# Bringing transposed value heads back in one DMA, and planning for a longer round trip

## The chip, the cores and the metric

The kernel runs on one core of a Trainium2 chip, in one launch. The metric is the device time of a run in microseconds (us). The kernel before takes 1620.33 us (median of 3 runs, 1620.0 to 1620.79).

The core has a matrix engine (TensorE, PE in the profile; its weight loads are listed as PEld), three engines for elementwise work (VectorE or DVE, ScalarE or ACT, GpSimd or POOL), and SyncE (SP), which here does nothing but issue DMAs. Each engine runs its own instructions in the order in which they stand in its program. A wait at the head of an engine's queue therefore holds up everything behind it.

## The reference

One layer of a decoder trunk on 512 tokens of width 1024, in float32:

```python
h = x + 0.5 * swiglu(rmsnorm(x, ffn1_norm), ffn1_w_in, ffn1_w_out)
h = h + hybrid_mixer(rmsnorm(h, mix_norm), w_in, ...)
h = h + 0.5 * swiglu(rmsnorm(h, ffn2_norm), ffn2_w_in, ffn2_w_out)
return rmsnorm(h, final_norm)
```

The mixer has one wide input projection whose columns feed two recurrent branches. The branch that matters here is Gated DeltaNet: 8 heads of queries and keys and 16 heads of values, each 128 wide. Values go through a causal convolution over 4 tokens and a SiLU, and then into a chunked delta rule:

```python
qkv = silu(causal_short_conv(concatenate([gq, gk, gv], -1), conv_w))
cq, ck, cv = split(qkv, [1024, 2048], -1)
# per value head, in chunks:
u = matmul(T, v * beta[..., None])
# scan over the chunks
v_new = u_c - w_c @ S
o = (q_c * exp(gam_c)) @ S + qk_c @ v_new
S = S * exp(g_end) + k_to_end.T @ v_new
```

The other branch (HGRN2, 8 heads) has a recurrence of its own. Both are projected back to 1024 columns, merged by sigmoid gates and projected once more.

## The kernel before, in words

**Stages.** The first feed-forward block takes the time up to about 362 us of the profiled span, the mixer runs to about 1265 us, and the second feed-forward block and the last norm take the rest. Every product is made of three float32r matmuls (high by high, high by low, low by high parts, L189 to L191), so each weight slab that arrives as `raw` is split by ACT into a high part (L1773) and by DVE into a low part (L1775).

**The mixer's order.** The mixer's instructions are put in order by a planner, the class `Desk`. The code is written as threads (Python generators). A thread asks for an engine for a stated time, for a buffer, for an event, or for a "lag", a time that passes in the plan without any engine. The planner runs its own clock and gives each engine to the waiting thread of the best rank. The order in which it serves the threads becomes the program order on every engine. The lags stand for transfers: `LAG["turn"]` for one way of a round trip through DRAM, `LAG["out"]` for a write to DRAM whose buffer comes free afterwards. A lag puts no wait into the program. The waits on the chip are semaphores that follow the data, whatever the plan thought.

**Threads.** `product` keeps PE busy with the dense projections. `loader` chooses which projection comes next, from a list (`DENSE`) as far as its needs are met, and otherwise from 16 gate products ("t"), which have no needs. It also holds back convolutions while seven of them are under way. The recurrence of head pair u (0 to 7) has the parts `g_n` (Gram products `pgq`, L1214), `g_b` (a triangular inverse of 32 by 32 blocks on POOL, which begins with four loads `gfs<-nb`, L1253), `g_inv` (the inverse of larger blocks, with transposes at L1284, L1291 and L1348), `g_w` (values times beta, L1273) and `g_rec` (the scan, which starts with the products `pw`, L1406).

**Values.** For each of the 16 value heads the projection leaves the head as 128 channels on the partitions by 512 tokens in a PSUM bank. `conv` takes two of the six buffers named `ta`, scales the product into one (`ci`, L1097), which frees the bank, and then convolves and applies the SiLU on ACT and DVE (L1102 to L1117). The scan wants tokens on the partitions. `turn` transposes blocks of 32 by 32 on DVE (L1126). `bounce` then writes the tile to DRAM (`vn<-ci`, 256 KB, L1132) and reads it back with the blocks in place (`gvb<-vn` or `x<-vn`, L1138): four DMAs of 64 KB, one for each group of 32 destination partitions. In both directions SP issues the DMAs, between the loads of weights (L1731) and the writes of other tiles (L1487, in `keep`). In the plan the `ta` buffer comes free after the first lag, and the head counts as finished after the second. `g_w` (L1273, on DVE) is the first reader.

The two banks for dense products (`mm`) are shared by all projections. The banks, the six `ta` buffers and the three buffers for `raw` are counted by the planner and guarded by semaphores on the chip.

Of the kernel before, what the change touches and what calls it, by code (L numbers as in the profile page):

```python
# [18 lines left out]
NT = T // P  # L19
# [29 lines left out]
STAY = (15,)  # L49
CONVS = 7  # L50
SLACK = 0.8
LAG = dict(raw=3.5, gb=6.5, nb=6, m=7, out=5, back=6, turn=2.5)
EASE = 2.5
LANES = {"a": 2, "b": 2, "d": 1, "e": 1}

# [632 lines left out]
def mixer(tc, mp, e):  # L688
    nc = tc.nc
    pe, act, dve, pool, sp = nc.tensor, nc.scalar, nc.vector, nc.gpsimd, nc.sync  # L690
# [73 lines left out]
    S = ("use", "SP", 0.4)  # L764
# [11 lines left out]
    def decays(pab):  # L776
# [74 lines left out]
        sp.dma_start(gtd, gt)  # L851
        yield "lag", LAG["out"]
        D.fire("decays")
# [237 lines left out]
    def conv(k, i, pt, out, n):  # L1091
# [21 lines left out]
        if n:  # L1113
            dve.scalar_tensor_tensor(out, a, 1.0, b, op0=ALU.add, op1=ALU.mult)
            D.put("ta", 2)
        else:
            dve.scalar_tensor_tensor(y, a, 1.0, b, op0=ALU.add, op1=ALU.mult)  # L1117
            yield V(512)
            turn(th, y)
            D.put("ta")  # L1120
            yield from bounce(f"vn{i}", th, out, "ta")
        D.fire(k)

    def turn(out, x):

        dve.transpose(out.rearrange("p (f c j) -> p c f j", f=4, c=NT), x)  # L1126

    def bounce(name, x, out, tag=None):

        yield S  # L1130
        scr = dr.tile([P, T], F32, name=name)
        sp.dma_start(scr, x)  # L1132
        yield "lag", LAG["turn"]
        if tag:
            D.put(tag)
        for f in range(4):
            yield S
            sp.dma_start(out[32 * f:32 * f + 32].rearrange("p (r a) -> p r a", r=4),  # L1138
                         scr.rearrange("(r i) (f a) -> f i r a", i=32, f=4)[f])
        yield "lag", LAG["turn"]  # L1140

    def g_e(u, st):
# [3 lines left out]
        for i in range(2):  # L1146
# [4 lines left out]
            act.dma_start(gb, gtd[hd_:hd_ + 1].rearrange("o (c b) -> o c b", c=NT).to_broadcast([P, NT, P]))  # L1151
            yield "lag", LAG["gb"]
            a = G["at"][u % 4 * 2 + i]
# [85 lines left out]
    def g_b(u, st):  # L1239
# [4 lines left out]
        for b in range(4):  # L1244
            r = slice(32 * b, 32 * b + 32)
            yield S
            sp.dma_start(nb[b].rearrange("s i j -> i s j"), n2[r, :, :, r].rearrange("p a c j -> p (a c) j"))
        yield "lag", LAG["nb"]
        yield "on", *([("P", u - 1)] if u else ["m"])
# [9 lines left out]
        sp.dma_start(t, eye4)  # L1259
        yield "lag", LAG["m"]  # L1260
        for j in range(31):
# [736 lines left out]
```

## Time and profile before

| | us |
|---|---|
| median of 3 runs | 1620.33 |
| lowest and highest | 1620.0 and 1620.79 |
| the profiled execution | 1619.26 |
| its span, first to last instruction | 1617.5 |
| outside the span | 1.76 |

A row of a group of instructions reads: engine, operation, out<-in by the program's names, count, then the durations in ns (least, median, most) and the first and last start. In a timeline the first two columns are start and duration in us, and a bracket at the end gives the idle time of the engine just ahead of the instruction and what ended it. In the table by windows each row is one stretch: its bounds, its length, the busy time of each engine with its instructions, the clock granted to TensorE as a share of full speed, the share of the DMA engines and GB/s. In a list of waits the columns are the total in us, the number of times, and the longest.

### The profile page before, as it was taken

The page shows a single profiled execution, that of the slowest core. Times are in us where ns is not written, and L with a number is a line of the kernel's source. Part 1 is how long each engine was busy: PE and PEld are TensorE (multiplying, and loading weights), DVE is VectorE, ACT ScalarE, POOL GpSimd, SP SyncE. Part 2 cuts the span into 40 slices and gives each one's busy share as a digit, 9 for nine tenths or more (in the row PEclk, how much of TensorE's full clock was granted, in tenths as well). Part 3 has the DMA queues.
Part 4 walks back from the last instruction along what each step waited for, and adds up shares of the span by engine and source line. Part 5 has one row for each costly group of instructions (what it writes and reads, how often), then busy time and mean ns, then how long its engine had stood idle before and what let it go on. Part 6 is the DMA issues. An engine that isn't in the chain of part 4 may idle for free.

```text
span 1617.5 us, 29307 instructions
## 1 busy us (share of the span) xinstructions
PE 1593.9 (99%) x10608; PEld 1380.8 (85%) x10608; DVE 1156.3 (71%) x2275; ACT 831.3 (51%) x1872; POOL 413.0 (26%) x725
## 2 busy tenths in 40 slices
PE   9999999999999999999998999999999999999997
PEld 8999998888888888888886787788888899999887
DVE  6888885447787788679887888765545788888433
ACT  5666664233434436456665665564324566667222
POOL 0211221001121121356555456600001121121001
PEclk9999999999999999999999999999999999999998
DMA  5777863332321322554343335446544587786333
GB/s 185 170 159 158 182 158 104 114 115 79 105 60 54 105 79 86 156 157 118 104 140 121 113 118 159 148 137 195 164 143 130 132 180 159 157 181 151 93 89 117
DMA packets 133345, 213.30 MB, mean 132 GB/s; under 512 B 22464, under 2 KB 36544, under 8 KB 133200
## 3 DMA queue, kind: packets, MB, share of 16 engines
q1 hardware_dynamic: 116208, 180.80, 37.2%
q0 software_dynamic: 14400, 26.22, 10.5%
q10 hardware_dynamic: 2592, 4.42, 0.9%
q8 instruction: 83, 1.36, 0.4%
q14 instruction: 62, 0.51, 0.1%
HBM read 192.21 MB, written 19.17 MB: 131 GB/s over the span
## 4 chain that ended last, share of the span: by engine, by line
PE 82%; DMA 8%; issue 6%; POOL 2%; DVE 1%; SPq 1%; ACT 1%; POOLq 0%; DVEq 0%; ACTq 0%
PE pmm L189 18%; PE pmm L190 17%; PE pmm L191 17%; PE px L191 5%; PE px L190 5%; PE px L189 5%; DMA wlo<-w1b 3%; DMA wlo<-w1a 2%; PE pnat L189 2%; PE pnat L191 2%; PE pnat L190 2%; PE pgq L1214 1%; DMA gvb<-vn 1%; PE pw L1406 1%; DMA vn<-ci 1%
## 5 line engine op out<-in xcount | busy, mean ns | idle before, releaser
L189 PE MATMUL pmm<-uh,whi 128*128 128x512 f32 x879 | 362.7, 413 | 3.1 <-DVE ci L1097 2.3
L191 PE MATMUL pmm<-uh,wlo 128*128 128x512 f32 x879 | 344.1, 391 | 0.0
L190 PE MATMUL pmm<-ul,whi 128*128 128x512 f32 x879 | 342.8, 390 | 0.0
L191 PE MATMUL px<-xs,wlo 128*128 128x256 f32 x1008 | 285.8, 284 | 1.2 <-DMA wlo<-w1b 0.6
L190 PE MATMUL px<-xs,whi 128*128 128x256 f32 x1008 | 285.3, 283 | 0.0
L189 PE MATMUL px<-xs,whi 128*128 128x256 f32 x1008 | 285.2, 283 | 0.0
L1773 ACT CAST whi<-raw 128x512 fp32r<-128x512 f32 x226 | 140.1, 621 | 231.3 <-PE pmm L190 182.1
L1775 DVE TENSOR_TENSOR wlo<-raw,whi 128x512 fp32r<-128x512 f32 x226 | 158.9, 705 | 108.8 <-ACT whi L1773 105.0
L191 PEld LDWEIGHTS pmm<-uh,wlo 128*128 128x128 f32 x879 | 165.4, 188 | 36.3
L189 PEld LDWEIGHTS pmm<-uh,whi 128*128 128x128 f32 x879 | 165.8, 189 | 35.4 <-DVE ci L1097 3.6
L191 PEld LDWEIGHTS px<-xs,wlo 128*128 128x128 f32 x1008 | 193.5, 192 | 2.2 <-DMA wlo<-w1b 1.3
L189 PEld LDWEIGHTS px<-xs,whi 128*128 128x128 f32 x1008 | 193.5, 192 | 0.1
L190 PEld LDWEIGHTS px<-xs,whi 128*128 128x128 f32 x1008 | 193.5, 192 | 0.1
L190 PEld LDWEIGHTS pmm<-ul,whi 128*128 128x128 f32 x879 | 166.1, 189 | 29.7 <-DVE ul L216 0.3
L329 ACT CAST whi<-sw 128x512 fp32r<-128x512 f32 x144 | 87.6, 613 | 92.7 <-DVE sw L366 72.7
L308 DVE TENSOR_TENSOR wlo<-raw,whi 128x512 fp32r<-128x512 f32 x100 | 77.6, 788 | 78.2 <-ACT whi L329 77.8
L329 ACT CAST whi<-raw 128x512 fp32r<-128x512 f32 x104 | 61.4, 592 | 127.4 <-PE pmm L190 91.7
L227 POOL TENSOR_TENSOR acc<-acc,sqt 128x512 f32<-128x512 f32 x18 | 23.4, 1300 | 320.2 <-ACT sqt L225 320.2
L308 DVE TENSOR_TENSOR wlo<-sw,whi 128x512 fp32r<-128x512 f32 x144 | 98.1, 681 | 0.0
L329 ACT CAST whi<-rw 128x512 fp32r<-128x512 f32 (+1 forms) x130 | 79.5, 613 | 26.5 <-PE px L190 14.5
L189 PE MATMUL pmm<-xs,whi 128*128 128x512 f32 (+1 forms) x238 | 89.8, 377 | 0.0
L190 PE MATMUL pmm<-xs,whi 128*128 128x512 f32 (+1 forms) x238 | 89.7, 377 | 0.0
(473 smaller groups left out, 3224.6 us busy)
## 6 DMA issues: line engine op xcount, KB each, us to landing
raw<-wt SPq DMA_DIRECT2D x160, 256.0 KB
rw<-w1b SPq DMA_DIRECT2D x80, 256.0 KB
rw<-w1a SPq DMA_DIRECT2D x74, 256.0 KB
wlo<-w1b POOLq DMA_DIRECT2D x53, 256.0 KB, 5.2
wlo<-w1a POOLq DMA_DIRECT2D x47, 256.0 KB, 5.2
raw<-w2b SPq DMA_DIRECT2D x41, 256.0 KB
raw<-w2a SPq DMA_DIRECT2D x36, 256.0 KB
raw<-wn SPq DMA_DIRECT2D x32, 256.0 KB
```

Of the source, the lines that this page charges most:

```text
L189: pe.matmul(pt, ah, bh, start=first, stop=False)
L190: pe.matmul(pt, ah, bl, start=False, stop=False)
L191: pe.matmul(pt, al, bh, start=False, stop=last)
L227: add.tensor_tensor(acc, acc, s, op=ALU.add)
L308: dve.tensor_tensor(lo, x, hi.bitcast(F32), op=ALU.subtract)
L329: act.copy(hi, x)
L1214: pe.matmul(pq[:, (c % 2) * 256:(c % 2) * 256 + 256], kq[:, c, 0], kq[:, c].rearrange("p a b -> p (a b)"), start=True, stop=True)
L1406: pe.matmul(pw[:, hd2[i]], ut[:, 4 * i + c], xs[i], start=True, stop=True)
L1773: act.copy(hi, raw)
L1775: dve.tensor_tensor(lo, raw, hi.bitcast(F32), op=ALU.subtract)
```

## The change

Three things change, all in the mixer.

1. `turn` reads the tokens in another order. Before, it took 32 neighbouring tokens to a block. Now it takes every fourth token of a chunk of 128, so the instruction reads with a step of four elements (16 bytes) where it read without a gap. The instruction, its size (128 by 512) and the way in which it writes are the same.
2. `bounce` reads back with one DMA of 256 KB over all 128 partitions where four DMAs of 64 KB each filled 32 partitions. The runs of the transfer are 128 elements (512 bytes) in both. With every fourth token in a block, the 128 destination partitions step evenly through the DRAM tile, so that one pattern describes them.
3. Two lags of the planner: `turn` from 2.5 to 7.5, used once for each way, and `out` from 5 to 6.5, used for every write of `keep` (outputs of heads, gates, branch products) and for the write of the decays.

The two patterns of the new `turn` list the sixteen blocks in different orders (the output by chunk and then by residue, the input by residue and then by chunk), so by the code as written chunk and residue change places between the blocks. The instructions, pieces and bytes are as many either way.

```diff
-LAG = dict(raw=3.5, gb=6.5, nb=6, m=7, out=5, back=6, turn=2.5)
+LAG = dict(raw=3.5, gb=6.5, nb=6, m=7, out=6.5, back=6, turn=7.5)
...
     def turn(out, x):
 
-        dve.transpose(out.rearrange("p (f c j) -> p c f j", f=4, c=NT), x)
+        dve.transpose(out.rearrange("p (f c j) -> p c f j", f=4, c=NT), x.rearrange("p (c i f) -> p f c i", c=NT, f=4))
...
         yield "lag", LAG["turn"]
         if tag:
             D.put(tag)
-        for f in range(4):
-            yield S
-            sp.dma_start(out[32 * f:32 * f + 32].rearrange("p (r a) -> p r a", r=4),
-                         scr.rearrange("(r i) (f a) -> f i r a", i=32, f=4)[f])
+        yield S
+        sp.dma_start(out.rearrange("p (r a) -> p r a", r=4), scr.rearrange("(r i) (f a) -> (i f) r a", r=4, f=4))
         yield "lag", LAG["turn"]
```

More of the change, by code (lines that the diff above doesn't have):

```diff
@@ L1124, in turn @@
     def turn(out, x):
-        dve.transpose(out.rearrange("p (f c j) -> p c f j", f=4, c=NT), x)
+        dve.transpose(out.rearrange("p (f c j) -> p f c j", f=4, c=NT), x.rearrange("p (c i f) -> p f c i", c=NT, f=4))
     def bounce(name, x, out, tag=None):
```

## The prediction

> **What bounds the kernel now.** I read the page first: its span, the table of busy time and the shares of the chain that ended last.
>
> ```profile
> span 1617.5 us, 29307 instructions
> ...
> PE 1593.9 (99%) x10608; PEld 1380.8 (85%) x10608; DVE 1156.3 (71%) x2275; ACT 831.3 (51%) x1872; POOL 413.0 (26%) x725
> ...
> PE 82%; DMA 8%; issue 6%; POOL 2%; DVE 1%; SPq 1%; ACT 1%; POOLq 0%; DVEq 0%; ACTq 0%
> ```
>
> TensorE is the bound, and all its idle time is 1617.5 - 1593.9 = 23.6 us. The change removes no matmul, so it can only win idle time or clock. Next, the table by windows, with the part of the mixer in which heads of values go through DRAM (640 to 1110) and the part behind it.
>
> ```profile
> 640.00:1110.00 470.00, 457.60 (x2828) 374.71 (x2827) 365.63 (x791) 269.51 (x771) 225.05 (x512) 0.99 0.44 133
> 1110.00:1265.00 155.00, 155.00 (x701) 128.71 (x700) 78.00 (x121) 58.08 (x103) 10.88 (x8) 1.00 0.54 165
> ...
> 1040.00:1060.00 20.00, 19.73 (x100) 16.46 (x99) 13.70 (x28) 10.82 (x30) 10.84 (x30) 1.00 0.71 205
> ```
>
> Idle here is 470 - 457.60 = 12.40 us; the end of the mixer has none. To see which of it hangs on the round trip, I took the list of waits (also of SP's queue), then the timelines of PE, DVE and ACT at the gaps.
>
> ```profile
> DVE gvb L1273 <- DMA gvb<-vn: 18.9, 7, 6.0
> ACT cy L1102 <- DMA vn<-ci: 7.3, 1, 7.3
> ...
> SPq L1731 <- DVE wlo L1775: 270.6, 108, 22.5
> SPq L1138 <- DMA vn<-ci: 28.0, 9, 6.2
> ```
>
> ```profile
> 678.83 1.10 PE L1214 MATMUL pgq<-h 128*128 128x256 f32 x4 [0.99 <-DVE gqm L1220]
> 881.97 2.08 PE L1214 MATMUL pgq<-h 128*128 128x256 f32 x4 [3.68 <-DVE gqm L1220]
> 1009.58 0.74 PE L1406 MATMUL pw<-x,x 128*128 128x128 f32 x4 [0.62 <-DVE x L1397]
> 1011.33 0.50 PE L189 MATMUL pmm<-uh,whi 128*128 128x512 f32 x1 [1.01 <-DVE ci L1097]
> 1022.78 0.75 PE L1406 MATMUL pw<-x,x 128*128 128x128 f32 x4 [1.61 <-DVE x L1397]
> ```
>
> ```profile
> 675.45 0.69 DVE L1273 TENSOR_TENSOR gvb<-gvb,sm 128x512 f32<-128x512 f32 x1 [5.99 <-DMA gvb<-vn]
> 879.00 0.69 DVE L1273 TENSOR_TENSOR gvb<-gvb,sm 128x512 f32<-128x512 f32 x1 [2.55 <-DMA gvb<-vn]
> 1019.38 0.73 ACT L1102 ACTIVATE cy<-ci,cs 128x512 f32<-128x512 f32 x1 [7.35 <-DMA vn<-ci]
> ```
>
> DVE sat 18.9 us, seven times, with the scaling of values (L1273) at its head, and ACT 7.35 us with a convolution whose buffer was still being written out. The plan had put both too early. Three PE gaps stand right behind such a wait: 0.99 us at 678.83, 3.68 at 881.97, 1.61 at 1022.78. The window at 1040 holds a fourth, 20 - 19.73 = 0.27 us. The gaps at 1009.58 and 1011.33 come before ACT's wait and don't belong to it.
>
> **How wrong the plan was.** The chain of waits shows one round trip whole, and the start of a second.
>
> ```profile
> 865.89 0.72 DVE ci L1126
> 866.67 5.76 DMA vn<-ci
> 872.49 0.33 SPq L1138
> ...
> 874.28 4.60 DMA gvb<-vn
> ...
> 915.38 0.71 DVE ci L1126
> ...
> 1012.69 6.59 DMA vn<-ci
> ```
>
> The write was issued at 866.67 and L1273 started at 879.00, 12.3 us later. The plan before allows, from the write's turn on SP, 0.4 + 2.5 + 4 x 0.4 + 2.5 = 7.0 us, which is 5.3 too short. The plan after allows 0.4 + 7.5 + 0.4 + 7.5 = 15.8, which is 3.5 too long.
>
> **Part 1, what the longer lags take away.** With 15.8 us, the planner puts other work ahead of L1273, so the four stalls should go.
> - At 678.83 the whole gap, 0.99. What stands next in DVE's order is a weight split that needed no value.
> - At 881.97, DVE without its idle 2.55 and the 0.69 of L1273 gives the mask (L1220) 3.24 earlier. Of 3.68 us, 0.44 stays, for PE then waits on the transposes and masks in the same queue.
> - At 1022.78, 1.61: `ta` counts as held for 7.5 us, above the 5.76 and 6.59 of the two writes shown, so ACT should find another buffer. The weight split behind it is next.
> - At 1040 to 1060, 0.27.
>
> The clock comes back with the second gap:
>
> ```profile
> 875.00:880.00 5.00, 2.16 (x55) 1.58 (x53) 2.45 (x5) 3.44 (x9) 4.06 (x13) 0.88 0.71 222
> 880.00:885.00 5.00, 3.03 (x7) 2.00 (x7) 4.65 (x12) 1.01 (x2) 4.14 (x12) 0.50 0.27 105
> 885.00:890.00 5.00, 5.00 (x37) 3.84 (x36) 2.88 (x5) 2.71 (x7) 4.29 (x10) 0.94 0.14 41
> 1010.00:1015.00 5.00, 3.99 (x13) 3.03 (x13) 3.66 (x10) 1.90 (x5) 0.00 (x0) 0.69 0.51 146
> ```
>
> Busy time by missing clock: 2.16 x 0.12 + 3.03 x 0.50 + 5.00 x 0.06 = 2.07 us. The dip to 0.69 at 1010 follows the other two gaps and stays out. [...]
>
> Part 1 is 0.99 + 3.24 + 1.61 + 0.27 + 2.07 = 8.18 us, bounded by 0 (every stall replaced by one as long).
>
> **Part 2, the strided transpose.**
>
> ```profile
> L1126 DVE STREAM_TRANSPOSE ci<-cy x16: 695/708/712, 661.4 to 1039.3; 128x512 f32<-128x512 f32 x16
> ...
> L1291 DVE STREAM_TRANSPOSE gut<-gtp x8: 425/437/442, 710.1 to 1024.2; 32x256 f32<-32x256 f32 x8
> ...
> L1348 DVE STREAM_TRANSPOSE gt<-gut x6: 301/302/305, 720.3 to 1032.8; 32x128 f32<-32x128 f32 x6
> ...
> L1284 DVE STREAM_TRANSPOSE x<-gln x3: 703/716/737, 749.6 to 1061.2; 128x256 f32<-128x256 f32 x3
> ```
>
> From 128 to 256 elements the time grows by 437 - 302 = 135 ns, which extended to 512 gives 437 + 270 = 707 ns, as L1126 has. L1284 reads with a step (8 elements) and writes with one, and takes 716 - 437 = 279 ns more for 256 elements: 1.09 ns an element, 0.56 us for 512. The row doesn't tell reads from writes, and the new `turn` has the read step only. Bounds: 0 and 0.56 us each; I take 0.28, half of what both sides cost. [...] DVE is busy 365.63 of 470 us here, and its slack covers most of the sixteen; where that cover is gone, all 16 cost 4.5 us (9.0 at most). The chain names two (865.89 and 915.38): +0.56 us, between 0 and 9.0.
>
> **Part 3, one DMA back.**
>
> ```profile
> L1138 SPq DMA_DIRECT2D gvb<-vn x48: 302/424/1026, 667.3 to 1045.6; - x48
> ```
>
> Three issues fewer at 0.424 us are 1.27 us of SP a head, 20.4 for sixteen. SP isn't the limit: it waited 270.6 us for weight splits alone, and those waits hide this gain. In the round trip above, one issue at 872.49 replaces a last one at 874.28, 1.79 us earlier. The transfer is four times as large: between 4.60 us (a quarter) and 6.59 (as many bytes, the slower write), so it lands between 1.8 earlier and 0.2 later. I take the middle, 0.8 earlier, worth nothing once the plan waits 15.8 us: 0. If packets of 512 bytes made it 4 x 4.60 = 18.4 us, that would be a rival.
>
> **Part 4, what the longer lags put later.** A scan can't start before its values. Three of the eight started right behind them:
>
> ```profile
> 826.95 0.76 DVE L1273 TENSOR_TENSOR x<-x,sm 128x512 f32<-128x512 f32 x1
> 928.69 0.69 DVE L1273 TENSOR_TENSOR gvb<-gvb,sm 128x512 f32<-128x512 f32 x1 [2.23 <-DMA gvb<-vn]
> 991.21 0.83 DVE L1273 TENSOR_TENSOR x<-x,sm 128x512 f32<-128x512 f32 x1
> ```
>
> ```profile
> 829.44 0.61 PE L1406 MATMUL pw<-x,x 128*128 128x128 f32 x4
> 931.51 0.61 PE L1406 MATMUL pw<-gvb,h 128*128 128x128 f32 x4
> 992.79 0.60 PE L1406 MATMUL pw<-x,x 128*128 128x128 f32 x4
> ```
>
> From the end of L1273 to `pw` it is 1.73, 2.13 and 0.75 us. The plan now puts these three starts up to 15.8 - 7.0 = 8.8 us later. Dense products cover that on PE, and the order of loads, gates and convolutions around them changes throughout, so some new gaps will come. I price one for each of the three at the mean of the three gaps around 1009 to 1023, (0.62 + 1.01 + 1.61) / 3 = 1.08: +3.24 us, between 0 and 3 x 3.68 = 11.0. The lag `out` has one term with this: it moves buffers and loads in the plan, and no wait for those writes is among those above; 0.
>
> **Sum.** -8.18 + 0.56 + 0 + 3.24 = -4.38 us. Against the profiled execution (1619.26, span 1617.5 and 1.76 around it) that is 1614.9; the median, 1620.33, stands 1.07 above that execution, so I forecast 1616.0.
>
> **Rivals.** About 0.2% (3.2 us) is what a measurement of this kernel tells from no change.
> - *The stalls only move.* For: the plan's order is new throughout, and three scans lose their start. If each costs a wait like DVE's two of 2.55 and 2.23 (mean 2.39), part 4 is 7.2 and the sum -8.18 + 0.56 + 7.2 = -0.4: 1619.9, no change. Against: the lag is long enough for the value to be there.
> - *Buffers run short, slower.* The place is `ta`: a convolution takes two of six before the instruction (L1097) that frees a PSUM bank, there are two banks, and the plan holds one buffer 5 us longer for each head. Products then stand behind L1097, as at 1011.33 (1.01 us). If the eleven heads from 5 on each cost that, +11.1: 1616.0 + 11.1 = 1627.1. It decides from 4.3 us on (0.4 a head), where the gain is gone. For: that gap exists already. Against: the chip holds the buffer for some 6 us in either kernel; only the order is new.
> - *The transpose is on the path everywhere*: 9.0 in place of 0.56, sum +4.1: 1624.4. Against: DVE's idle fifth.
> - *The change doesn't do what it says*: at 18.4 us a transfer, the value lands 5.8 + 0.4 + 18.4 = 24.6 us after its write is issued, 8.8 past the plan's 15.8, and DVE waits 7 x 8.8 = 62 us where it waited 18.9. Those 18.9 us cost PE 0.99 + 3.24 + 0.27 + 2.07 = 6.57; scaled by 62 / 18.9 that is 21.6, so the sum is 21.6 - 6.57 - 1.61 + 0.56 + 3.24 = +17.2: 1637.5.
>
> **Chances and range.** Forecast 0.42 (its own range 1611 to 1617), stalls move 0.22 (1617 to 1623.5), buffers 0.26, transposes 0.06, slow transfer 0.04. So faster by over 0.2% 0.42, within 0.2% 0.22, slower 0.36. The range reaches from the full gain, 1620.33 - 8.18 - 1 for what else may fall away, 1611, to 1630, past the buffer rival's 1627.1 and part 4's upper bound (-8.18 + 0.56 + 11.0 = +3.4).
>
> **What would show it.** Right: DVE's waits at L1273 fall from 18.9 us to under 3, ACT's at L1102 to 0, PE's idle time in this part from 12.40 to about 8, with no window at half clock; L1138 has 16 issues; L1126 takes about 0.99 us. Wrong: new PE gaps behind L1097 (buffers), behind L1397 or the masks (moved stalls), L1126 at 1.27 and DVE above 85% (transposes), or waits at L1273 that stay (transfer).

## The result and the profile after

The changed kernel takes 1606.07 us (median of 4 runs, 1604.59 to 1610.05), the kernel before 1620.16 (median of 4 runs, 1618.16 to 1620.79). The ratio is 0.9919 (95% interval 0.9899 to 0.9939), so the change saves about 14 us. The profiled execution took 1606.94 us, 12.3 less than that of before. The direction was forecast, the size was not: -4.4 us were forecast, and the time lies 5 us below the lower end of the range.

**A correction to the section on the change.** The diff was misread there in one point. The output pattern of the new `turn` is "p f c j", not "p c f j":

```diff
-        dve.transpose(out.rearrange("p (f c j) -> p c f j", f=4, c=NT), x)
+        dve.transpose(out.rearrange("p (f c j) -> p f c j", f=4, c=NT), x.rearrange("p (c i f) -> p f c i", c=NT, f=4))
```

Both patterns of the new line go by residue and then by chunk, so the blocks keep their places. The way of writing does change: before, the output was written in block steps, and now without a gap. The paragraph that lets chunk and residue change places is void. The counts and sizes given there hold.

First the page of the changed kernel: its span, the busy times, and the shares of the chain that ended last.

```profile
span 1605.2 us, 29206 instructions
...
PE 1589.0 (99%) x10608; PEld 1380.3 (86%) x10608; DVE 1163.2 (72%) x2275; ACT 831.0 (52%) x1872; POOL 417.5 (26%) x725
...
PE 88%; DMA 4%; issue 3%; DVE 3%; ACT 1%; POOL 0%; POOLq 0%; SPq 0%; DVEq 0%; ACTq 0%
```

TensorE's idle time fell from 23.6 us to 1605.2 - 1589.0 = 16.2, which is 7.4 of the 12.3. The other 4.9 is busy time: the same 10608 matmuls took 1589.0 where they took 1593.9. The clock has a part in that. These are the mean granted clocks, first of the kernel before, then of the one after:

```profile
core 0: 1617.5 us, clock 0.994
```

```profile
core 0: 1605.2 us, clock 0.997
```

0.003 of 1600 us is 4.8 us. So the gain has two parts, fewer gaps and a clock that dips less. How much the clock gives is known only roughly: the four runs of the changed kernel have mean clocks of 0.994 to 0.998, with times of 1610.05 to 1604.59 us. In the mixer 1.8 us of it can be located, behind gaps (3.46 us before, 1.70 after, by the measure that the experiments use). Nor is all of the 12.3 the mixer's: its last product ended at 1255.7 us before and at 1244.9 after, 10.8 earlier, and the other 1.5 lie behind it, where nothing was changed. The table by windows of the changed kernel shows the same two stretches as before:

```profile
640.00:1110.00 470.00, 465.07 (x2881) 384.76 (x2881) 377.20 (x800) 274.50 (x782) 230.94 (x513) 1.00 0.45 136
1110.00:1265.00 155.00, 154.47 (x695) 127.46 (x694) 81.29 (x123) 61.12 (x103) 12.74 (x11) 1.00 0.54 162
```

Idle in the first is 470 - 465.07 = 4.93 us, where it was 12.40. The waits at the first reader of the values (now L1271), in the list of waits:

```profile
DVE gvb L1271 <- DMA gvb<-vn: 0.5, 1, 0.5
```

DVE's 18.9 us are now 0.5, ACT's 7.3 at L1102 are gone, and so are SP's 28.0 at the read-back but for 1.9:

```profile
SPq L1552 <- DMA vn<-ci: 6.5, 2, 4.9
SPq L1137 <- DMA vn<-ci: 1.9, 2, 1.7
```

In exchange there is a new wait of 6.5 us at L1552, a load of `og` into a buffer that a write of values still holds. It leads to the one large gap that is left. The timeline of PE has two gaps over 0.4 us in the mixer:

```profile
807.92 0.50 PE L189 MATMUL pmm<-uh,whi 128*128 128x512 f32 x1 [0.85 <-DVE ci L1097]
...
1014.79 0.70 PE L1391 MATMUL pks<-s,h 128*128 128x256 f32 x2 [4.08 <-DVE s L1431]
```

The chain that ended last, in order of time (start, duration, what), tells how the second came about:

```profile
1002.98 6.97 DMA vn<-ci
...
1010.02 2.98 DMA og<-od
...
1013.02 0.63 ACT sogm L1558
1013.65 0.02 issue
1013.67 0.23 DVE soqm L1560
...
1014.40 0.34 DVE s L1431
```

The write of a head took 6.97 us. SP stood at L1552 until it had landed, `og` came in at 1013.0, ACT took its high part and DVE its low part, and the state of the scan (L1431) stood behind that subtraction in DVE's queue. PE waited for the state.

### The profile page after: what moved, and what is told of

Same layout as the page of the kernel before. It is cut to its first block, busy times and chain, and to the rows that moved or that the text cites. A ratio compares the mean times of both kernels' runs of the same rounds, so it can differ in the third digit from the quotient of the medians.

```text
span 1605.2 us, 29206 instructions
## 1 busy us (share of the span) xinstructions
PE 1589.0 (99%) x10608; PEld 1380.3 (86%) x10608; DVE 1163.2 (72%) x2275; ACT 831.0 (52%) x1872; POOL 417.5 (26%) x725
## 4 chain that ended last, share of the span: by engine, by line
PE 88%; DMA 4%; issue 3%; DVE 3%; ACT 1%; POOL 0%; POOLq 0%; SPq 0%; DVEq 0%; ACTq 0%
PE pmm L189 19%; PE pmm L190 18%; PE pmm L191 18%; PE px L191 5%; PE px L190 5%; PE px L189 5%; DMA wlo<-w1a 2%; PE pnat L189 2%; PE pnat L191 2%; PE pnat L190 2%; PE pgq L1212 1%; PE pw L1404 1%; PE pog L1420 1%; DMA wlo<-w1b 1%; PE pks L1392 1%
```

## The experiments

Two theories stood against each other. By the first, the *order* carries the gain: the longer lag makes the planner put other work ahead of whatever waits for the round trip. By the second, the *transfer* does: one DMA and the strided transpose make the round trip itself shorter or lighter. Below, "idle" is TensorE's idle time from 640 to 1260 us, 620 less the busy time in the table by windows. "Clock" is busy time by missing clock, summed over windows of 5 us. Of the kernel before these are 12.40 and 3.46 us, of the changed kernel 5.46 and 1.70, the 1.70 behind its gap of 4.08 us.

### Order and transfer apart

*The changed order with the old transfer.* All engines but SP have the changed kernel's order. Four DMAs stand where the one stood, and the transpose is the old one. Against the changed kernel:

```diff
-        dve.transpose(out.rearrange("p (f c j) -> p f c j", f=4, c=NT), x.rearrange("p (c i f) -> p f c i", c=NT, f=4))
+        dve.transpose(out.rearrange("p (f c j) -> p c f j", f=4, c=NT), x)
...
         yield S
-        sp.dma_start(out.rearrange("p (r a) -> p r a", r=4), scr.rearrange("(r i) (f a) -> (i f) r a", r=4, f=4))
+        [sp.dma_start(out[32 * f:32 * f + 32].rearrange("p (r a) -> p r a", r=4), scr.rearrange("(r i) (f a) -> f i r a", i=32, f=4)[f]) for f in range(4)]
```

> The order of instructions of the changed kernel on PE, ACT, POOL and DVE, with the four DMAs and the gapless transpose of the kernel before (SP issues the four where the one stood). Theory (the gain of 14 us comes from the order that the longer lags give): within 3 us of the changed kernel, 1603 to 1609. Rival 1 (the gain comes from the single transfer, which frees 1.27 us of SP a head and lands sooner): most of the gain is lost, 1613 to 1620. Rival 2 (the order alone, by chance and not by the size of the lag) expects the same as the theory here.

Measured: 1605.71 us (1605.01 to 1607.31), ratio 0.9915 (0.9893 to 0.9938), idle 3.28, clock 0. That is the whole gain without the new transfer, as the theory had it.

*The old order with the new transfer.* The one DMA stands where the last of the four stood. Against the kernel before:

```diff
-        dve.transpose(out.rearrange("p (f c j) -> p c f j", f=4, c=NT), x)
+        dve.transpose(out.rearrange("p (f c j) -> p f c j", f=4, c=NT), x.rearrange("p (c i f) -> p f c i", c=NT, f=4))
...
         for f in range(4):
             yield S
-            sp.dma_start(out[32 * f:32 * f + 32].rearrange("p (r a) -> p r a", r=4),
-                         scr.rearrange("(r i) (f a) -> f i r a", i=32, f=4)[f])
+        sp.dma_start(out.rearrange("p (r a) -> p r a", r=4),
+                     scr.rearrange("(r i) (f a) -> (i f) r a", r=4, f=4))
```

> The order of instructions of the kernel before, with the single DMA (issued where the fourth one stood) and the strided transpose. Theory: DVE still waits for values about 19 us in sum, and the time stays at that of before, 1618 to 1623 (the transposes cost up to 0.4 us each where they are on the path). Rival 1 (transfer): 1606 to 1612.

Measured: 1619.96 us, ratio 1.0002 (0.9989 to 1.0015), idle 13.16, clock 5.66. DVE still waits for the values. The list of waits of this kernel:

```profile
DVE gvb L1273 <- DMA gvb<-vn: 16.9, 6, 5.0
...
SPq L1138 <- DMA vn<-ci: 2.6, 2, 2.0
```

The second line shows something that the theory didn't ask for. SP's wait at the read-back is 2.6 us where it was 28.0, since the one DMA stands where the last of four stood, and the time is the same. From 640 to 1110 us SP's waits for weight splits (L1731 behind L1775) grew from 144.1 to 180.9 us instead. So nothing was gained with SP's wait gone, though the transposes were longer as well.

*The lags alone, and the transfer alone with its own plan.* The kernel before with the diff's line of `LAG` only:

```diff
-LAG = dict(raw=3.5, gb=6.5, nb=6, m=7, out=5, back=6, turn=2.5)
+LAG = dict(raw=3.5, gb=6.5, nb=6, m=7, out=6.5, back=6, turn=7.5)
```

> The kernel before with the lags of the changed one (turn 7.5, out 6.5) and nothing else; the plan still counts four turns of SP for the way back, so its order is not that of the changed kernel. Theory: waits of DVE for values under 3 us and a time of 1604 to 1611. Rival 1 (transfer): 1617 to 1623. Rival 2 (chance of an order): anything from 1604 to 1625, with the waits for values gone all the same.

The other way round, the changed kernel with the old line of `LAG`:

> The changed kernel with the lags of the kernel before (turn 2.5, out 5); the plan counts one turn of SP for the way back, so values are expected even sooner, 5.8 us after the write. Theory: DVE waits for values 19 us or more, and the time is 1618 to 1625. Rival 1 (transfer): 1606 to 1612. Rival 2 (chance): anything from 1604 to 1625.

Measured: the lags alone give 1603.53 us (1602.34 to 1604.31), ratio 0.99 (0.9878 to 0.9922), idle 1.63, clock 0. The transfer alone gives 1616.73 (1614.46 to 1620.16), ratio 0.9982 (0.997 to 0.9995), idle 9.86, clock 3.81, with 14.8 us of waits left at L1271 (19 or more and at least 1618 us were expected). Its plan has three steps of SP fewer for each head, so its order isn't that of before, and with the order of before the same transfer gave nothing. The transfer theory falls for all but some 0.2%.

*The strided transpose.* The changed kernel with the old way of reading, in the same order. The tokens stay as they were, so the blocks that come back hold other tokens than the scan takes them for; the work is as much:

```diff
-        dve.transpose(out.rearrange("p (f c j) -> p f c j", f=4, c=NT), x.rearrange("p (c i f) -> p f c i", c=NT, f=4))
+        dve.transpose(out.rearrange("p (f c j) -> p c f j", f=4, c=NT), x)
```

> The changed kernel with a transpose that reads without a gap (tokens then stand in another order, which it leaves as it is), so in the order of the changed kernel on every engine. The transpose goes from 1.10 to 0.71 us, 16 x 0.39 = 6.2 us of DVE. Theory (DVE's slack covers it): 1604 to 1608, no difference to the changed kernel. Rival (it is on the path): up to 6 us faster, 1600 to 1603.

Measured: 1606.83 us (1604.84 to 1607.83), ratio 0.9916 (0.9901 to 0.9932), idle 3.43. In all, the strided reads cost nothing that can be measured. In one place they can be seen. This is DVE's timeline of the changed kernel, and behind it that of this one, at the gap near 808:

```profile
806.10 1.15 DVE L1126 STREAM_TRANSPOSE ci<-cy 128x512 f32<-128x512 f32 x1
807.16 0.70 DVE L1097 TENSOR_TENSOR ci<-pmm,rbc 128x512 f32<-128x512 f32 x1
```

```profile
806.73 0.71 DVE L1126 STREAM_TRANSPOSE ci<-cy 128x512 f32<-128x512 f32 x1
807.38 0.68 DVE L1097 TENSOR_TENSOR ci<-pmm,rbc 128x512 f32<-128x512 f32 x1
```

L1097 stands right behind the transpose and frees a PSUM bank. PE's gap there is 0.85 us with the step and 0.41 without.

### Which lag, and which way

Four edits of the kernel before, in its line of `LAG` or in one of the two `yield "lag", LAG["turn"]` of `bounce`:

```diff
# the round trip's lag alone
+LAG = dict(raw=3.5, gb=6.5, nb=6, m=7, out=5, back=6, turn=7.5)
# the lag of the other writes alone
+LAG = dict(raw=3.5, gb=6.5, nb=6, m=7, out=6.5, back=6, turn=2.5)
# the write's way alone, the first lag of bounce
-        yield "lag", LAG["turn"]
+        yield "lag", 7.5
# the read's way alone, the second lag of bounce
-        yield "lag", LAG["turn"]
+        yield "lag", 7.5
```

> The kernel before with the lag of the round trip alone at 7.5 (writes of keep stay at 5). Theory (the time follows the waits for values that a plan leaves in the queues of DVE and ACT): waits for values on DVE under 3 us, 1602 to 1608. Rival (the lag for other writes carries part of the gain): 1609 to 1617.

> The kernel before with the lag for other writes alone at 6.5 (round trip stays at 2.5 each way). Theory: DVE still waits 15 to 25 us for values, 1615 to 1624. Rival (the other writes): 1603 to 1612. Rival (chance of an order): a gain of over 8 us with the waits still there.

> The kernel before with 7.5 for the write alone (read back 2.5, other writes 5), so that the plan allows 0.4 + 7.5 + 1.6 + 2.5 = 12.0 us where the chip took 12.3, and holds the buffer of the write long enough. Theory: ACT's wait of 7.3 us gone, DVE's waits for values from 18.9 to under 6, 1603 to 1610.

> The kernel before with 7.5 for the read back alone (write 2.5, other writes 5): again 12.0 us for the whole, but the plan issues the read-back on SP and frees the buffer too early. Theory: SP waits for the write at the read-back (28 us before) as it did, with the loads of weights behind it, and ACT may still wait for a buffer: DVE's waits under 6, and a time between the others, 1606 to 1615. If only the value's arrival counts, the same as with the write alone.

| lags (write, read; out) | us | ratio (interval) | idle, clock | DVE waits for values | SP waits for the write |
|---|---|---|---|---|---|
| before (2.5, 2.5; 5) | 1620.16 | | 12.40, 3.46 | 18.9 | 28.0 |
| both ways (7.5, 7.5; 5) | 1604.53 | 0.9899 (0.9884 to 0.9914) | 1.11, 0 | 0.6 | 0.4 |
| `out` (2.5, 2.5; 6.5) | 1620.71 | 1.0002 (0.9993 to 1.0011) | 12.85, 4.09 | 17.5 | 27.3 |
| write (7.5, 2.5; 5) | 1614.26 | 0.9961 (0.9947 to 0.9976) | 9.76, 2.75 | 12.0 | 0.4 |
| read (2.5, 7.5; 5) | 1621.54 | 1.001 (1.0001 to 1.002) | 14.51, 6.23 | 0 | 22.2 |

The lag `out` carries nothing, and the two ways of the round trip carry everything. Each way of the lag takes away one wait and leaves the other. With the write's way, SP no longer stands at the read-back, but DVE still meets values that aren't there: 12.0 us, where under 6 and 1603 to 1610 were expected. With the read's way DVE's waits are gone and nothing is gained, where 1606 to 1615 were expected. SP still stands 22.2 us at the read-back, but what can be seen to cost PE is something else. A single gap of 6.86 us stands behind a `ta` buffer that was taken too early (the next section shows the same gap at 5 and 5). With the clock lost in the three windows behind it (3.79 x 0.50 + 5.00 x 0.50 + 5.00 x 0.05 = 4.65 us) it takes back 11.5.

### The size of the lag

On the kernel before, with `out` at 6.5 and `turn` at 5 or 10:

> The kernel before with 5 each way (other writes 6.5). The plan allows 0.4 + 5 + 1.6 + 5 = 12.0 us for the whole, as in the two runs with one way at 7.5 (1614.3 and 1621.5), but 5 for the write, where the trace shows 5.8 to 6.6. Theory (each way has a wait of its own: SP and the buffers wait for the write, DVE for the value): both waits are left, but small, SP under 10 us at the read-back and DVE under 8, 1606 to 1613. If only the sum of both ways counted, 1614 to 1621.

> The kernel before with 10 each way (other writes 6.5), 22.0 us for the whole. Theory: no waits for values or writes, as at 7.5, and the gain is kept, 1602 to 1608; a longer lag costs only if scans start so late that PE runs out of products. Rival (part 4 of the prediction: later scans leave gaps): 1609 to 1618. Rival (7.5 is a lucky order): any time from 1604 to 1620 with no waits on transfers.

With `out` at 5 and `turn` at 7 or 8:

> The kernel before with 7 each way (other writes 5). Theory (size of the lag): 1602 to 1609, waits for writes and values under 3 us each. Lucky order at 7.5: 1609 to 1622.

> The kernel before with 8 each way (other writes 5). Theory (size of the lag): 1602 to 1610, waits for writes and values under 2 us each. Lucky order at 7.5: 1609 to 1622.

And with one way at 7.5 and the other at 5:

> The kernel before with 7.5 for the write and 5 for the read back (14.5 us in all with the turns of SP; other writes 5). Theory (the write's lag must be above the 5.8 to 7.0 us that writes took, and the sum above 12.3 to 13.3): no wait of SP for a write at the read-back, no gap behind L1097 of over 3 us, DVE's waits for values under 4: 1602 to 1609. Chance of an order: 1603 to 1620.

> The same sum the other way round: 5 for the write, 7.5 for the read back. Theory: SP waits some 10 us at the read-back and a buffer is taken too early, with a PE gap behind L1097 of 2 to 7 us; no waits of DVE at L1273: 1610 to 1623. If only the sum counts, 1602 to 1609.

| lags (write, read) | us | ratio (interval) | idle, clock | DVE waits for values | SP waits for the write |
|---|---|---|---|---|---|
| 5, 5 | 1622.84 | 1.0021 (1.001 to 1.0032) | 12.09, 7.34 | 5.1 | 10.0 |
| 5, 7.5 | 1613.65 | 0.9958 (0.9943 to 0.9973) | 8.89, 1.53 | 0 | 1.5 |
| 7.5, 5 | 1613.51 | 0.9955 (0.9939 to 0.9972) | 7.39, 3.14 | 0.6 | 0.4 |
| 7, 7 | 1605.73 | 0.9907 (0.9892 to 0.9922) | 2.11, 0 | 0 | 1.0 |
| 8, 8 | 1610.64 | 0.9939 (0.9924 to 0.9954) | 4.95, 4.43 | 0 | 0 |
| 10, 10 | 1610.75 | 0.9942 (0.9928 to 0.9957) | 6.79, 1.45 | 0 | 0 |

At 7 each way and with 5 for the write and 7.5 for the read the time came out as expected, though in the latter SP waited 1.5 us for writes and not some 10. At 5 and 5, at 10, at 7.5 and 5 and, by 0.6 us, at 8 it was longer than the theory had it.

At 5 and 5 one gap of 7.05 us outweighs the waits that are gone. The timelines of SP, DVE and PE there:

```profile
962.70 0.60 SPq L1132 DMA_DIRECT2D vn<-ci  x1
963.57 0.33 SPq L1731 DMA_DIRECT2D raw<-wt  x1
969.72 1.74 SPq L1138 DMA_DIRECT2D x<-vn  x4
```

```profile
969.70 0.68 DVE L1097 TENSOR_TENSOR ci<-pmm,rbc 128x512 f32<-128x512 f32 x1 [3.71 <-issue]
969.72 0.06 DVE L1096 MEMSET ci<- 128x3 f32 x1
```

```profile
970.44 0.79 PE L189 MATMUL pmm<-uh,whi 128*128 128x512 f32 x1 [7.05 <-DVE ci L1097]
```

The write went out at 962.70 and had landed at 969.7, after 7.0 us. At that moment both SP's read-back and DVE's L1097 started. In the program the small memset of L1096, which stands with L1097 at the start of a convolution, waits for the DMA that empties its `ta` buffer. (The trace names nothing that ended DVE's 3.71 us; that it was this write is read from the common moment.) The plan had that buffer free after 5 us. So the convolution couldn't start, the PSUM bank of the finished product wasn't freed, and PE stood. With the read's way alone the same gap is 6.86 us, at 971.21. Behind the gap the table by windows shows the clock:

```profile
965.00:970.00 5.00, 0.00 (x0) 0.00 (x0) 1.29 (x4) 2.67 (x11) 1.15 (x5) 0.57 0.54 186
970.00:975.00 5.00, 4.56 (x40) 3.37 (x41) 2.97 (x11) 0.54 (x2) 4.07 (x10) 0.50 0.18 52
975.00:980.00 5.00, 5.00 (x15) 3.95 (x14) 1.41 (x4) 2.31 (x4) 4.06 (x13) 0.56 0.13 29
```

It costs 4.56 x 0.50 + 5.00 x 0.44 = 4.48 us more.

From 7 us on DVE doesn't wait over 1.0 us in all for a value, nor SP at the read-back, and yet 8 and 10 are 5 to 6 us slower than 7 and 7.5, and the mixed pairs of 5 and 7.5 are 8 to 9 slower. Most of their gaps stand behind other things. This is PE's part of the list of waits with 7.5 and 5, and behind it with 10 and 10:

```profile
PE pmm L189 <- ACT uh L1477: 3.1, 2, 1.5
PE pmm L189 <- DVE ci L1097: 1.3, 3, 0.8
PE pks L1393 <- DVE s L1429: 1.2, 1, 1.2
PE pog L1420 <- ACT ptk L1175: 1.1, 1, 1.1
```

```profile
PE pks L1393 <- DVE s L1433: 3.3, 2, 3.1
PE pmm L189 <- ACT uh L1477: 1.5, 1, 1.5
```

`uh` of L1477 is the high part of the last scans' normed output. The waits of 3.1 and 1.5 us for it stand at the end of the scans, where dense products no longer covered that. The 3.1 us behind L1433 at 10 and 10 do belong to a transfer of values, as DVE's timeline there shows:

```profile
968.88 0.69 DVE L1513 TENSOR_TENSOR zg<-pmm,rbc 128x512 f32<-128x512 f32 x1 [4.24 <-DMA vn<-ci]
```

DVE waited 4.24 us for a write of a head that held the buffer which L1513 wanted, and the state of the scan stood behind L1513 in DVE's queue. So even a lag of 10 didn't keep a write from being late, for the plan's times and the chip's had drifted apart by then. At 8 and 8 the gaps of 1.72 us at 960 and 1.33 at 963 ended with work of DVE (L1411 and L1097), and the table has no wait of DVE for a value or of SP for a write.

### A control: another order for another reason

How far does the time move when the planner's order changes and the round trip does not? `EASE`, a lag that the planner leaves at seven other places and none of them in the round trip, from 2.5 to 2.6, on the kernel before:

```diff
-EASE = 2.5
+EASE = 2.6
```

> Control: the kernel before with another allowance of the plan changed a little (EASE, for small powers on POOL, from 2.5 to 2.6), which puts the whole mixer into another order and leaves the round trip as it was. Theory: DVE waits 14 to 25 us for values and SP 20 us or more for writes, 1616 to 1626. Rival (any new order gains): 1603 to 1612.

Measured: 1634.52 us (1631.48 to 1634.73), ratio 1.0084 (1.0068 to 1.0101), idle 21.65, clock 6.57. That is slower than either theory had it. Another order moves the time by as much as the change did, here to the slower side, with the transfer waits still in it:

```profile
DVE gvb L1273 <- DMA gvb<-vn: 24.2, 7, 6.3
DVE x L1273 <- DMA x<-vn: 4.7, 2, 4.3
PE pmm L189 <- DVE zg L1513: 3.8, 2, 2.1
```

DVE's waits for values are 28.9 us here, 10 more than before. So part of the 14.6 us may be these waits and not the order as such.

**What the runs settle, and what stays open.** That the order from the round trip's lag carries the gain is shown: with it and without the rest the gain is whole, and with the rest and without it the gain is nothing or 0.2%. That both lags had to be long is shown by the two ways apart. The write's lag governs two waits, SP's at the read-back and the next user's of the buffer. No run parts them, but the old order with one DMA, where SP's wait was gone and nothing was gained, and the gaps of 7 us behind L1097 speak for the buffer. How much of the 14 us is the waits and how much a lucky order is settled in part. Of the six lags that took both waits to under 2 us each (5 and 7.5; 7.5 and 5; 7; 7.5; 8; 10), all are faster than the kernel before of the same round, by 6.9 to 15.9 us. So some 7 us come with the long lags in every order seen. The further 8 to 9 us of 7 and 7.5 come with those two orders, and no run tells whether that is a merit of these lags or chance.

The fastest kernels seen are the kernel before with the lag alone: 1603.53 us with both lags and 1604.53 with `turn` alone. Their intervals (0.9878 to 0.9922, 0.9884 to 0.9914) overlap that of the changed kernel (0.9899 to 0.9939), so a version better than both isn't shown.

## Why the prediction was right or wrong

**The mechanism was right.** The longer lag takes the value waits away. DVE's waits at L1273 went from 18.9 to 0.5 us (under 3 was forecast), ACT's from 7.3 to 0, the read-back became 16 issues (L1137), and PE's idle time from 640 to 1110 us fell to 4.93, further than the "about 8" that was named. One sign failed in part: there still is a window below full clock, though not at half of it, at 1015:

```profile
1010.00:1015.00 5.00, 0.92 (x34) 0.79 (x34) 2.94 (x7) 1.93 (x5) 4.06 (x13) 1.00 0.70 212
1015.00:1020.00 5.00, 5.00 (x47) 3.71 (x47) 4.11 (x9) 2.26 (x9) 4.37 (x9) 0.66 0.57 186
```

**Part 1 was mis-sized; this is the step that failed.** It priced 8.18 us, and with the lag alone on the kernel before, 11.29 us of idle time and all 3.46 of clock went, 14.75 in all. It counted only gaps that stand right behind a named wait for the values: 6.11 us of idle time and 2.07 of clock. The gaps at 1009 and 1011 and the dip behind them were set down as not belonging to the round trip, and four more were passed over. The timeline of PE of before has these:

```profile
778.44 0.70 PE L1393 MATMUL pks<-s,h 128*128 128x256 f32 x2 [0.84 <-DVE s L1429]
...
867.38 0.50 PE L189 MATMUL pmm<-uh,whi 128*128 128x512 f32 x1 [0.76 <-DVE zg L1513]
...
877.61 0.68 PE L1331 MATMUL pq<-gut,gn 64*64 64x64 f32 x16 [1.13 <-ACT gut L1321]
...
916.76 0.50 PE L189 MATMUL pmm<-uh,whi 128*128 128x512 f32 x1 [1.33 <-DVE ci L1097]
```

All six were taken as staying. None of them is in the changed kernel, nor in the kernel with the lag alone. With what was left of the gap at 882 and smaller ones they are 12.40 - 6.11 = 6.29 us of idle time and 1.39 of clock, so the term could have been 15.9 and not 8.2. That gaps go when the order is new doesn't show what had caused them, and the trace of before gives little reason to put them down to late values. Ahead of the gaps at 867, 916, 1009 and 1011 DVE was busy with other work (masks, splits, transposes). Its last wait at L1273 had ended 23 us earlier at 916, and 80 us or more earlier at 778, 867 and 1009. Only the gap at 877 falls into such a wait. So the prediction read most of these gaps rightly. What it missed is that an order that is new throughout doesn't keep the old order's gaps: it let new ones come (part 4) and old ones stay. That the new order had so few of its own was in part luck, as far as the control and the lags of 8 and 10 tell. How much of the 6.29 hung on the late values in a less direct way is not settled.

What the time by execution adds up to is open in part too. Of the profiled 12.3 us, 6.94 are idle time in the mixer and 1.76 clock behind its gaps. The 1.5 behind the mixer and 2.1 of busy time in it that no window below full clock shows are in no term.

**Part 3 was right, term and reason, as far as one run shows.** The one DMA is worth nothing, as forecast, and SP isn't the limit: in the old order with one DMA 25.4 of its 28.0 us at the read-back went, its waits for weight splits grew by 36.8, and the time stayed. The longer transposes of that run cost 1.2 us in the three gaps named under part 2, so a gain of that size could be hidden. As for the transfer, these are rows of the chain of the kernel with the old order and one DMA:

```profile
889.07 4.62 DMA gvb<-vn
...
1046.21 5.00 DMA gvb<-vn
```

A single 256 KB read took 4.62 and 5.00 us here, about the fourth's 4.60 and inside the bounds of 4.60 and 6.59. In the changed kernel one took 3.2 (issued at 880.6, by its time to landing), so the lower bound was too high.

**Part 2 was right where it mattered.** The group of transposes after:

```profile
L1126 DVE STREAM_TRANSPOSE ci<-cy x16: 1071/1100/1146, 661.3 to 1041.8; 128x512 f32<-128x512 f32 x16
```

Each takes 1.10 us, 0.39 more than before: above the 0.28 taken, below the bound of 0.56. In the old order with the strided transpose the two that the forecast named can be seen: the gap at 867 grew from 0.76 to 1.18 us and that at 917 from 1.33 to 1.71, 0.80 where 0.56 was forecast, and the one at 1011 grew too, from 1.01 to 1.39. In the changed order one is left, which costs PE 0.85 - 0.41 = 0.44 us at 808. The new transpose reads with a step and also writes in another way; the row doesn't tell which of the two the 0.39 us belong to.

**Part 4 was too small, though within its bounds, and had another reason.** It priced three later scan starts at 1.08 us each, 3.24. The changed kernel has new gaps of 4.08 and 0.85 us and a clock loss of 1.70, 6.63 in all. The large one isn't a late scan start: the chain above shows a load behind a buffer that a write holds. With the lag alone on the kernel before, it isn't there at all. Late last heads, which part 4 may have had in mind, would show at the end of the scans, as the 1.5 us at a lag of 10 and 3.1 at 7.5 and 5 do; that later values caused these isn't shown.

**The rivals.** "Buffers run short" named a real mechanism, L1097 behind a `ta` buffer, and got its sign wrong: the gaps of 7 us come where the plan frees the buffer too early (2.5 or 5 us for a write of 7.0). A longer lag doesn't end this altogether: a buffer held by a write costs once in the changed kernel, at L1552, and once at a lag of 10, at L1513. "The stalls only move", "the transpose on the path everywhere" and "the change doesn't do what it says" didn't come.

## What to carry to other kernels

With a planner's order on in-order queues, a lag that was too short made waits here at every queue that the late transfer headed: the issuer (28.0 us on SP), the reader (18.9 on DVE) and the next user of the buffer (a gap of 7 us on PE at once). Not every such wait cost time: SP's 28.0 could go without a gain. Give such a lag the longest transfer that the traces show, and not the middle one: writes of the same 256 KB took 2.7 to 7.0 us here. Lags of 7 us and more each way gained in all runs, by 9 to 16 us, and which of them is best was not settled. When the order is new throughout, don't take the old gaps as staying, whatever released them, and price a new order by itself with a spread: here a change of 0.1 in a constant moved the time by 14 us.

## What the runs showed of the hardware that wasn't expected

The clock's dip behind a gap didn't follow the gap's length alone. In the run with the write's lag alone, gaps of 1.83 us at 680 and 2.00 at 831 left the clock at 1.00, and one of 1.90 at 866 took its window to 0.68. A gap of 4.08 us cost 1.70 us of clock and one of 7.05 cost 4.48. In the same order as the changed kernel, a gap of 2.33 us left the clock at 1.00 and one of 2.49 took it to 0.81 and 0.85:

```profile
1010.00:1015.00 5.00, 2.67 (x42) 2.10 (x41) 3.29 (x9) 3.32 (x10) 4.29 (x10) 1.00 0.96 305
1015.00:1020.00 5.00, 5.00 (x56) 4.10 (x55) 4.78 (x11) 2.79 (x8) 4.29 (x10) 1.00 0.20 64
```

```profile
1010.00:1015.00 5.00, 2.51 (x39) 1.92 (x37) 3.73 (x9) 3.17 (x9) 4.28 (x9) 0.81 0.98 297
1015.00:1020.00 5.00, 5.00 (x51) 3.93 (x50) 3.46 (x9) 1.77 (x8) 4.16 (x11) 0.85 0.27 74
```

The first is the kernel with four DMAs, the second that with the old transpose. What besides the length sets the dip isn't shown.

The round trip's transfers scatter widely. Where the chains of these runs show one, a write of 256 KB to DRAM took 2.65 (old order with one DMA, at 741) to 6.97 us (changed kernel, at 1003) until it had landed. A read of the same bytes in one DMA took 3.2 (changed kernel, at 881) to 5.00 (old order with one DMA, at 1046). Why the longer ones took longer isn't shown.
